# Sums of weights formed in DRAM, and six up-projection tiles in seven products, in a hybrid transformer block

## The chip, the cores and the metric

The kernel runs on one core of a Trainium2 chip. The metric is device time in microseconds (us) of one execution, the median of several runs. Engines are called by their short names in the profile: PE is TensorE, DVE is VectorE, ACT is ScalarE, POOL is GpSimd, and SP is SyncE, which only issues transfers (DMAs).

## The reference

One layer on 512 tokens of width 1024, all in float32:

```python
h = x
hn = rms_norm(h, ln_mix);  z = hn @ w_in            # 1024 x 3590
o_a = diff_attention(...)        # 4 heads, ALiBi, chunk-causal, difference of two softmaxes
o_b = forgetting_attention(...)  # 6 heads, causal, cumulative log forget gate
o_c = chunk_attention(...)       # 6 heads, own and earlier chunks, relative bias
h = h + concat(o_a, o_b, o_c) @ w_out               # 1024 x 1024
u = rms_norm(h, ln_ffn) @ w_up                      # 1024 x 5632
c = conv_b + sum_j conv_w[j] * shift(u, 2 - j)      # causal, width 3, along the tokens
gate, val = split(c)                                # 2816 features each
h = h + (silu(gate) * val) @ w_down                 # 2816 x 1024
g = sigmoid(rms_norm(h, ln_ple) @ w_ple_gate)       # 1024 x 1024
out = h + (p @ w_ple_proj) * g
```

## The kernel before

Every float32 product is made of three matmuls on operands that are split into a high part (`hi`, float32r) and a rest (`lo`): hi*hi, hi*lo and lo*hi (`mm3`). A weight tile is loaded into a raw tile of 128 x 768 (or 512) floats; ACT copies it to `w_hi`, DVE subtracts that from the raw tile and writes `w_lo` (`split`).

**Attention.** A loop over the parts of `w_in` (A0b, A1, A1b, B0, B1, B2, C0, C1, C2) runs four units each, one for 128 tokens, and then eight units of the output projection (`wo`, half n = 0, then n = 1). These units are counted by `slot`, 4 to 47. Between the matmuls of a unit stand pieces of the attention of earlier heads, by a table of slots (`T`). PE's order is that of the program; the other engines are ordered by the tile framework's planner, which simulates a time line, unless an instruction is pinned. `prefetch` loads the weights of the next part at the end of a unit. Some rests are formed by DMA: ACT writes the negated high part and GpSimd's queue adds the raw tile to it (`B_l<-B_r`, `C_l<-C_r`, `wo_l<-wo_r`).

**MLP.** A feature tile f (0 to 21) is 128 gate features and 128 value features. Plain tiles (`up_plain`) take three raw tiles (768, 768, 512 columns) and 48 matmuls of 512 tokens. Tiles in `SEVEN` (5, 10, 15) are computed by a scheme with seven products of half-size blocks in place of eight (`up_seven`), 84 matmuls of 256 columns, from weights that are sums of blocks: 3584 columns in five raw tiles. The right sides (sums of normalized columns, `Xh`, `Xl`) are formed once. After a tile come the convolution taps, the silu and the product with the value (`ff_chain`), all on ACT and DVE. Two finished tiles make one `left`: the seven sums of halves that the down projection multiplies (`g_ah`, `g_al`, or `xh`, `xl` at the end).

The down projection runs in phases of 6, 6, 6 and 4 feature tiles (`PHASES`) and, in each, for two halves n of the columns, again in seven products (`Down.product`, `RIGHT`, `PRODUCTS`), which are accumulated in three PSUM banks X, Y, Z; DVE adds each to `h` (`add_h`). Phases 0 and 1 run between up tiles, phases 2 and 3 together at the end (d0 and d1), followed by the gate (`pg`).

**The sums of weights.** They are formed in SBUF. For an up tile in seven products, five raw tiles are loaded, GpSimd's queue adds further blocks by three accumulating loads (`add_of`) and GpSimd adds four pairs of blocks (`sum_of`). For a down phase and half four blocks are loaded (`a1`, `b1`, `b2`, `a2`), and GpSimd forms the four differences `t1` to `t4` between the products, in the raw tiles (`diff`).

**Order in the MLP.** Each piece is a `Task` with its engines and estimated times. PE's tasks keep the order in which they are written; the others are ordered by a small planner that knows rings of buffers (`raw` 6, `hi` 7, `conv` 10, `left` 3), latest times counted back from PE and a clock per engine. Loads are emitted as soon as what they depend on is emitted, in a fixed order, and SP executes them in that order. The order of up tiles and down products comes from `fill`, `downs` and `AHEAD`.

## Time and profile before

| | |
|---|---|
| time, median of 3 runs | 728.63 us (727.79 to 728.96) |
| the profiled execution's own time | 727.37 us |
| its span, first to last instruction | 725.6 us |
| granted TensorE clock, mean | 0.999 |
| PE / DVE / ACT / POOL busy | 705.8 / 556.3 / 394.1 / 267.3 us |
| HBM read / written | 74.19 / 4.21 MB |

In the profile an instruction is named by what it writes and reads, `out<-in,in`; L78 is the line of the helper through which most engines are called, so instructions are told apart by their tiles. `w_raw`, `w_hi`, `w_lo` are weight tiles, `u` the up products, `sX`, `sY`, `sZ` the banks of a tile in seven products, `dn_X`, `dn_Y`, `dn_Z` those of the down projection, `dn_a`, `dn_b`, `dn_t` the raw tiles of its last phase. A group's row gives the count behind x, then busy us, the mean ns of one, the idle time of the engine before them and what ended it. A queue's row gives packets, MB and the share of the time of 16 DMA engines.

### The profile page before, as it was taken

Reading aid. Unit: us, or ns where it says so; the run is one execution under the profiler, and the core shown is the slowest. Engines: PE = TensorE matmul, PEld = TensorE weight load, DVE = VectorE, ACT = ScalarE, POOL = GpSimd, SP = SyncE. Lnnn points to the kernel's source line nnn. Section 1 sums busy time; section 2 is a strip of 40 time slices with the busy share of each in tenths; the row PEclk is TensorE's granted clock in tenths of the full one; section 3 lists DMA queues with packets and bytes.
Section 4 is the critical chain, followed back from the end, with each engine's and each line's share of the span. In section 5 each row is a group of like instructions: output and inputs, shape, how many; then the busy total and the mean of one; then the engine's idle time right before and its main releaser. Section 6 shows DMA issues by size and latency. Waiting matters only on the chain. (4 is left out here: it accounts for less than half of the span.)

```text
span 725.6 us, 11877 instructions
## 1 busy us (share of the span) xinstructions
PE 705.8 (97%) x4218; PEld 632.3 (87%) x4218; DVE 556.3 (77%) x1091; ACT 394.1 (54%) x745; POOL 267.3 (37%) x355
## 2 busy tenths in 40 slices
PE   9998999999999999999999999999999999999997
PEld 8888989898999887889888899888998888899886
DVE  7678788887878855758879968787898779988552
ACT  6656775865766664565555544543444543544821
POOL 5676676756665640211101144031520004361400
PEclk9999999999999999999999999999999999999999
DMA  9454425514211135564545334552263322122531
GB/s 330 170 139 110 124 59 124 138 30 110 88 53 52 59 66 167 170 208 90 144 138 125 101 97 122 142 156 66 88 178 114 95 87 83 57 73 93 159 126 58
DMA packets 36950, 83.22 MB, mean 115 GB/s; under 512 B 4214, under 2 KB 6262, under 8 KB 36892
## 3 DMA queue, kind: packets, MB, share of 16 engines
q1 hardware_dynamic: 32844, 73.52, 32.4%
q0 software_dynamic: 3760, 8.66, 6.4%
q8 instruction: 33, 0.54, 0.3%
q10 hardware_dynamic: 288, 0.30, 0.1%
q14 instruction: 25, 0.20, 0.1%
HBM read 74.19 MB, written 4.21 MB: 108 GB/s over the span
## 5 line engine op out<-in xcount | busy, mean ns | idle before, releaser
L78 DVE TENSOR_TENSOR w_lo<-w_raw,w_hi 128x768 fp32r<-128x768 f32 (+1 forms) x118 | 114.4, 989 | 20.2 <-ACT w_hi L78 19.6
L78 ACT CAST w_hi<-w_raw 128x768 fp32r<-128x768 f32 (+1 forms) x118 | 89.6, 786 | 70.1 <-POOL w_raw L78 32.0
L78 PE MATMUL u<-Tl,w_hi 128*128 128x512 f32 (+1 forms) x336 | 125.5, 374 | 0.8 <-DVE Tl L78 0.8
L78 PE MATMUL u<-Th,w_hi 128*128 128x512 f32 (+1 forms) x336 | 125.6, 374 | 0.6 <-ACT pps L78 0.6
L78 PE MATMUL u<-Th,w_lo 128*128 128x512 f32 (+1 forms) x336 | 125.3, 373 | 0.0
L78 POOL TENSOR_TENSOR w_raw<-w_raw,w_raw 128x768 f32<-128x768 f32 (+1 forms) x30 | 54.3, 1833 | 145.2 <-DVE w_lo L78 113.8
L78 PEld LDWEIGHTS u<-Tl,w_hi 128*128 128x128 f32 x336 | 63.0, 188 | 13.1 <-DVE Tl L78 1.2
L78 PEld LDWEIGHTS u<-Th,w_hi 128*128 128x128 f32 x336 | 63.0, 188 | 12.9 <-ACT pps L78 1.0
L78 PEld LDWEIGHTS u<-Th,w_lo 128*128 128x128 f32 x336 | 63.0, 188 | 12.5
L78 DVE SCALAR_TENSOR_TENSOR c<-u,cols,c 128x511 f32<-128x511 f32 x76 | 56.6, 746 | 18.6 <-ACT c L78 17.4
L78 POOL DMA_DIRECT2D w_raw<-in_w_up_dram x9 | 7.9, 907 | 100.1 <-DMA w_raw<-in_w_up_dram 93.9
L78 ACT ACTIVATE c<-u,cols 128x512 f32<-128x512 f32 x38 | 29.5, 776 | 22.7 <-PE u L78 22.7
L78 PE MATMUL dn_X<-w_hi,g_ah 128*128 128x256 f32 x144 | 40.7, 282 | 0.3 <-DVE h L78 0.3
L78 PE MATMUL dn_X<-w_lo,g_ah 128*128 128x256 f32 x144 | 40.6, 282 | 0.3 <-DVE w_lo L78 0.3
L78 PE MATMUL dn_X<-w_hi,g_al 128*128 128x256 f32 x144 | 40.5, 281 | 0.0
L78 PE MATMUL B_z<-B_h,Th 128*128 128x384 f32 x96 | 34.5, 360 | 0.6 <-DVE B_zn L78 0.6
L78 PE MATMUL C_z<-C_h,Th 128*128 128x384 f32 x96 | 34.3, 357 | 0.0
L78 PE MATMUL B_z<-B_h,Tl 128*128 128x384 f32 x96 | 32.3, 337 | 0.0
L78 PE MATMUL B_z<-B_l,Th 128*128 128x384 f32 x96 | 32.3, 337 | 0.0
L78 PE MATMUL C_z<-C_h,Tl 128*128 128x384 f32 x96 | 32.3, 336 | 0.0
L78 PE MATMUL C_z<-C_l,Th 128*128 128x384 f32 x96 | 32.3, 336 | 0.0
L78 PEld LDWEIGHTS dn_X<-w_hi,g_ah 128*128 128x128 f32 x144 | 27.1, 188 | 0.9 <-ACT w_hi L78 0.5
(484 smaller groups left out, 2143.8 us busy)
## 6 DMA issues: line engine op xcount, KB each, us to landing
w_raw<-in_w_up_dram SPq DMA_DIRECT2D x50, 384.0 KB, 3.9
w_raw<-in_w_down_dram SPq DMA_DIRECT2D x24, 384.0 KB, 3.1
w_raw<-in_w_up_dram SPq DMA_DIRECT2D x22, 256.0 KB, 3.3
B_r<-in_w_in_dram SPq DMA_DIRECT2D x12, 384.0 KB, 3.1
C_r<-in_w_in_dram SPq DMA_DIRECT2D x12, 384.0 KB, 3.3
wo_r<-in_w_out_dram SPq DMA_DIRECT2D x16, 256.0 KB, 3.0
w_raw<-in_w_ple_gate_dram SPq DMA_DIRECT2D x16, 256.0 KB, 3.0
h<-in_x_dram SPq DMA_DIRECT2D x4, 512.0 KB, 7.7
```

Of the source, the lines that this page charges most:

```text
L78: ins = getattr(self.eng, op)(*a, **k)
```

## The change

The sums of weights are formed in DRAM, by DMA alone. For each of ten sums (an up tile in seven products, or a down phase) a DRAM tile of four blocks is filled by four copies from the inputs (`copy_sum`, on SP's queue, in slots 8 to 43 of the attention) and three accumulating transfers from GpSimd's queue (`add_sum`: two blocks get the other addends, then block 1 is added to block 0, and block 0 to block 3). The sums that are needed first (up tiles 4, 7, 9 and phase 0) are added in slots 22 to 38, the others behind feature tiles 0 to 15 in the MLP (`late_sum`), each after a one-column GpSimd operation on the finished tile. The MLP then loads finished sums: `sum_of`, `add_of`, `again` and `diff` are gone, and a down phase and half loads seven raw tiles instead of four.

Six up tiles (4, 7, 9, 11, 13, 15) are computed in seven products instead of three (5, 10, 15). The order of up pieces (P plain, S seven) and down products (D) in the MLP is written out as a string. The seven products of the down projection use sums with other signs and in another order, with `add_h` adding or subtracting, and the left sums follow. `pool` and `sp` name the same engines as `nc.gpsimd` and `nc.sync`, through a wrapper that remembers the last instruction. The inputs hold the blocks in a matching layout (`w_usum`, `w_dsum`, `w_dadd`).

```diff
-AHEAD = 2
-SEVEN = (5, 10, 15)
+ORDER = ("PPPPSSPSSSPSPPPPSSPSSSPSPSSPSSSPSPDDDDDDDDDDDDDDSSPSSSPSPSSPSSSPSPSSPSSSPSPDDDDDDDDDDDDDDPPPPPPPPPPPPPPPPP")
+def tiles_of(order):
+    f, n, tiles = 2, {"P": 0, "S": 0}, {"P": [], "S": []}
+    for c in order:
+        if c in n:
+            if n[c] == 0:
+                tiles[c].append(f)
+                f += 1
+            n[c] = (n[c] + 1) % {"P": 3, "S": 6}[c]
+    assert f == NF and not any(n.values()), (f, n)
+    return tiles["P"], tiles["S"]
+EARLY_SUMS, FIRST_SUM, LAST_SUM = 11, 22, 16
+PLAIN, SEVEN = tiles_of(ORDER)
+_sums = sorted([(f, "u", f) for f in SEVEN] + [(PHASES[ph + 1] + 3, "d", ph) for ph in range(len(PHASES) - 1)])
+COPIES, ADDS, LATE = {}, {}, {}
+_late = [q for q in _sums if q[0] >= EARLY_SUMS]
+for _i, _q in enumerate(_sums):
+    for _k in range(4):
+        COPIES.setdefault(8 + (4 * _i + _k) * 36 // (4 * len(_sums)), []).append((_q[1:], _k))
+for _i, _q in enumerate(q for q in _sums if q not in _late):
+    for _k in range(3):
+        ADDS.setdefault(FIRST_SUM + _i // 3 * 10 + _i % 3 + 3 * _k, []).append((_q[1:], _k))
+for _i, _q in enumerate(_late):
+    for _k in range(3):
+        LATE.setdefault((3 * _i + _k) * LAST_SUM // (3 * len(_late)), []).append((_q[1:], _k))
...
+    DSUM, USUM, SUMS = {}, {}, {}
+    def sums_of(key):
+        if key not in SUMS:
+            if key[0] == "d":
+                ph = key[1]
+                DSUM[ph] = dp.tile([P, 4, 2, w_down[ph].shape[4]], F32, tag=f"dsum{ph}", name=f"dsum{ph}")
+                SUMS[key] = DSUM[ph], w_dsum[ph], w_dadd[ph]
+            else:
+                f = key[1]
+                USUM[f] = dp.tile([P, 4, 512], F32, tag=f"usum{f}", name=f"usum{f}")
+                SUMS[key] = USUM[f], w_usum[f], w_up[f][:, 1024:2048].rearrange("p (i c) -> p i c", i=2)
+        return SUMS[key]
+    def copy_sum(key, k):
+        v, src, _ = sums_of(key)
+        with tc.issue_after(sp.last):
+            nc.sync.dma_start(out=v[:, k], in_=src[:, k])
+    def add_sum(key, k):
+        v, _, more = sums_of(key)
+        to, src = ((v[:, 1:3], more), (v[:, 0], v[:, 1]), (v[:, 3], v[:, 0]))[k]
+        pool.dma_start(out=to, in_=src, accum_op=ALU.add, max_dma_last_dim=6144)
+    def next_job():
+        for q in COPIES.get(slot, ()):
+            copy_sum(*q)
+        for q in ADDS.get(slot, ()):
+            with tc.issue_after(pool.last):
+                add_sum(*q)
...
             slot += 1
+            next_job()
...
-    PRODUCTS = ((L1A, 0, "X", True), (L1, 4, "Y", True), (L2, 5, "X", False), (L4, 2, "Y", False),
-                (L3, 6, "X", False), (L2A, 1, "Z", True), (L2B, 3, "X", False))
+    PRODUCTS = {"1e": (0, "X", True, 1, 0, ALU.add), "S1": (3, "Y", True, 0, 1, ALU.subtract), "S2": (4, "X", False, 0, 0, ALU.add),
+                "1o": (2, "Z", True, 1, 0, ALU.add), "1e2e": (5, "X", False, 0, 1, ALU.subtract), "1oS2": (1, "Y", False, 0, 0, ALU.add),
+                "2o": (6, "X", False, 1, 1, ALU.subtract)}
...
-        ws = [tile_of(n, f"ws{f}_{i}", w_up[f][:, 768 * i : 768 * i + n]) for i, n in enumerate(size)]
-        src = w_up[f]
-        a = [add_of(ws[2], 512, 768, lambda: src[:, 1024:1280]), add_of(ws[3], 0, 768, lambda: src[:, 1280:2048])]
-        sums = [(2, 0, 2, 512), (2, 256, 3, 0), (3, 256, 2, 512), (3, 512, 3, 0)]
-        a += [sum_of(ws[i], c0, ws[j], c1, H, a) for i, c0, j, c1 in sums]
-        b = [add_of(ws[4], 0, 512, lambda: src[:, 2048:2560])]
-        for w, deps in zip(ws, ((), (), a, a, b)):
-            split_of(w, deps)
-        order = (0, 1, 4, 3, 5, 6, 2)
+        usum = USUM[f].rearrange("p i c -> p (i c)")
+        ws = [tile_of(n, f"ws{f}_{i}", w_up[f][:, 768 * i : 768 * i + n] if i < 2 else usum[:, 768 * (i - 2) : 768 * (i - 2) + n],
+                      deps=SUM_TASKS.get(("u", f), ()) if i > 1 else ()) for i, n in enumerate(size)]
+        for w in ws:
+            split_of(w)
+        order = (0, 1, 4, 3, 6, 5, 2)
...
-        raw = {what: tile_of(m, f"{name}_{what}", src.get(what), tag) for what in ("a1", "b1", "b2", "t2", "a2")}
...
+        src = {f"{c + 1}{'eo'[i]}": w_down[ph][n, i, c] for i in range(2) for c in range(2)}
+        src.update({what: DSUM[ph][:, i, n] for i, what in enumerate(("S2", "S1", "1e2e", "1oS2"))})
+        return lambda what: split_of(tile_of(m, f"{name}_{what}", src[what], tag, SUM_TASKS.get(("d", ph), ()) if what in ("S2", "S1", "1e2e", "1oS2") else ()))
...
+        for q in LATE.get(len(done_f) - 1, ()):
+            late_sum(f, *q)
...
+    LAST_X, SUM_TASKS = [], {}
+    tok = mp.tile([P, 1], F32, tag="tok", name="tok")
+    def late_sum(f, key, k):
+        b, slot = done_f[f]
+        def do():
+            pool.tensor_scalar(tok, G[f][:, 0:1], 1.0, 1.0, ALU.mult, ALU.mult)
+            add_sum(key, k)
+        SUM_TASKS.setdefault(key, []).append(Task("add", [("pool", 1.2), ("acc", (6, 4, 4)[k] + (8 if key[0] == "d" else 3))], do, (b, *SUM_TASKS.get(key, ())), (), [slot]))
...
+    FIRST = ("1e", "S1", "1o"), ("1e", "S1")
+    def down_pieces():
         for ph in range(2):
-            if ph not in due and all(f in done_f for f in range(PHASES[ph], PHASES[ph + 1])):
-                due[ph] = 0
-
-    def fill(n):
-        for _ in range(n):
-            at_f[0] = next(plain, NF)
-            pieces[0] += 1
-            if pieces[0] % 3 == 0:
-                count()
-
-    def downs(after=3):
-
-        for ph in range(2):
-            if due.get(ph, -1) >= after:
-                due[ph] = -99
-                for n in range(2):
-                    down(ph, n, DT)
-
-    for f in SEVEN:
-        while at_f[0] < f - AHEAD:
-            fill(1)
-            if pieces[0] % 3 == 0:
-                downs()
-        for i, _ in enumerate(up_seven(f)):
-            if i in (1, 4, 5):
-                fill(1)
-        count()
-        downs()
-    while at_f[0] < NF:
-        fill(1)
-        if pieces[0] % 3 == 0:
-            downs()
-    downs(0)
+            for n in range(2):
+                d = Down((ph,), n, DT)
+                for what in PRODUCTS:
+                    d.product(what)
+                    yield
+        for n, whats in enumerate(FIRST):
+            DL.append(Down((2, 3), n, ({"X": "z", "Y": "s", "Z": "o"} if n else DT)))
+            for what in whats:
+                DL[n].product(what, (2,), False)
+                yield
+    DL = []
+    pieces = {"P": (f for f in PLAIN for _ in up_plain(f)), "S": (f for f in SEVEN for _ in up_seven(f)), "D": down_pieces()}
+    for c in ORDER:
+        next(pieces[c])
...
+    d0, d1 = DL
+    for what in PRODUCTS:
+        d0.product(what, (3,) if what in FIRST[0] else None)
+    d1.product("1e", (3,))
     cols3(0, 0)
     cols3(1, 0)
-    d1.product("a1", (3,))
+    d1.product("S1", (3,) if "S1" in FIRST[1] else None)
     cols3(2, 0)
-    d1.product("a2")
     cols3(3, 0)
-    for what in ("t1", "t2", "b2", "t3"):
+    for what in ("S2", "1o", "1e2e", "1oS2"):
         d1.product(what)
+    d1.product("2o")
     cols3(0, 1)
     cols3(1, 1)
-    d1.product("t4")
```

131 lines of the change are left out of this document (42 added, 89 removed).

## The prediction

> **What bounds the kernel now.** I read the share of each engine first, then the stretches by stage, then who made TensorE wait, then the chain of the work that ended last. The first rows are the engines over the whole span; below them each row is one stretch: its length, the busy time of each engine, the granted clock, the DMA engines' mean busy share and GB/s.
>
> ```profile
> span 725.6 us, 11877 instructions
> PE 705.8 (97%) x4218; PEld 632.3 (87%) x4218; DVE 556.3 (77%) x1091; ACT 394.1 (54%) x745; POOL 267.3 (37%) x355
> ...
> core 0: us, PE busy (x) PEld busy (x) DVE busy (x) ACT busy (x) POOL busy (x), PEclk, DMA share, GB/s
> 60.00:115.00 55.00, 51.50 (x336) 47.94 (x335) 44.54 (x122) 38.27 (x86) 36.53 (x51) 1.00 0.47 119
> 115.00:230.00 115.00, 113.14 (x694) 107.09 (x693) 94.55 (x305) 76.26 (x184) 74.33 (x114) 1.00 0.29 81
> 230.00:290.00 60.00, 58.71 (x308) 50.07 (x307) 37.80 (x94) 34.67 (x80) 23.65 (x35) 1.00 0.34 92
> 325.00:430.00 105.00, 105.00 (x595) 91.02 (x595) 85.10 (x122) 56.30 (x85) 18.41 (x18) 1.00 0.43 112
> 430.00:460.00 30.00, 30.00 (x254) 29.96 (x253) 24.47 (x32) 12.42 (x17) 9.64 (x5) 1.00 0.52 155
> 460.00:515.00 55.00, 55.00 (x281) 46.17 (x280) 43.94 (x63) 27.74 (x42) 12.33 (x10) 1.00 0.36 96
> 515.00:545.00 30.00, 29.66 (x250) 29.49 (x249) 26.45 (x33) 12.32 (x17) 9.89 (x5) 1.00 0.52 156
> 545.00:620.00 75.00, 75.00 (x327) 60.40 (x326) 62.41 (x86) 34.02 (x51) 10.16 (x5) 1.00 0.32 96
> 620.00:676.00 56.00, 53.72 (x445) 52.63 (x444) 48.16 (x61) 26.70 (x42) 20.05 (x11) 1.00 0.24 76
> ```
>
> TensorE is the bound nearly everywhere, at full granted clock. From 325 to 676 us, the MLP, it is busy for all but 0.34 us (515 to 545) and 2.28 us (620 to 676). So a matmul taken out of the MLP is time gained, as long as nothing else becomes late. The attention (60 to 290) loses 3.50 + 1.86 + 1.29 = 6.65 us, and GpSimd is busy there for 74.33 of 115 us in the long middle stretch: the room for new work of its own is smallest in that place.
>
> **The products.** The change turns six feature tiles instead of three into seven-product tiles. The chain gives the price of each kind of matmul:
>
> ```profile
> 545.45 50.41 PE u L78 x216
> ...
> 646.02 5.30 DVE w_lo L78 x3
> ...
> 660.27 3.56 PE dn_X L78 x30
> ```
>
> A 128x512 product (u) takes 50.41 / 216 = 0.2334 us, a 128x256 one (dn_X, the shape of the seven products too) 3.56 / 30 = 0.1187 us. A plain up tile is 2 halves x 8 blocks x 3 products of 512 columns, 48 x 0.2334 = 11.20 us. A seven-product tile is 7 x 4 x 3 = 84 of 256 columns, 9.97 us. Each tile that moves saves 1.23 us, three save 3.7 us. The number of down products stays (7 per phase and half); only their order and signs change. Nothing covers these matmuls, so I count the whole 3.7.
>
> **GpSimd's sums and VectorE beside them.** The change removes from the MLP every sum and difference of weights that GpSimd forms in SBUF, and the nine accumulating loads of raw tiles. What these cost now is to be seen on VectorE. Forms of 325 to 676 us on VectorE (count, busy us, mean ns), GpSimd's accumulating loads (ns least/median/most), and single instructions in order of time:
>
> ```profile
> L78 DVE TENSOR_TENSOR w_lo<-w_raw,w_hi 128x768 fp32r<-128x768 f32 x87 | 92.2, 1076 | 12.3 <-ACT w_hi L78 11.9
> L78 DVE TENSOR_TENSOR w_lo<-dn_a,w_hi 128x512 fp32r<-128x512 f32 x8 | 8.4, 1058 | 0.5 <-ACT w_hi L78 0.3
> L78 DVE TENSOR_TENSOR sm<-c 128x256 f32<-128x256 f32 x11 | 6.3, 569 | 0.1
> L78 DVE TENSOR_TENSOR su<-sX,su 128x256 f32<-128x256 f32 x12 | 4.8, 419 | 8.4 <-ACT su L78 8.3
> ...
> L78 POOL DMA_DIRECT2D w_raw<-in_w_up_dram x9: 857/872/1185, 326.0 to 474.2; - x9
> ...
> 601.50 2.06 DVE L78 TENSOR_TENSOR sm<-c 128x256 f32<-128x256 f32 x1
> 622.79 0.42 DVE L78 TENSOR_TENSOR sm<-c 128x256 f32<-128x256 f32 x1
> 613.36 0.69 DVE L78 TENSOR_TENSOR c<-c,c 128x512 f32<-128x512 f32 x1
> 612.49 0.95 DVE L78 TENSOR_TENSOR w_lo<-w_raw,w_hi 128x768 fp32r<-128x768 f32 x1
> 613.96 2.61 DVE L78 TENSOR_TENSOR w_lo<-w_raw,w_hi 128x768 fp32r<-128x768 f32 x1
> 613.57 2.18 POOL L78 TENSOR_TENSOR w_raw<-w_raw,w_raw 128x768 f32<-128x768 f32 x1 [8.29 <-issue]
> ```
>
> The same low-half subtraction takes 0.95 us alone and 2.61 us beside a GpSimd sum; `sm` 0.42 and 2.06. So VectorE waits for GpSimd's sums. Over the MLP that is 87 x (1.076 - 0.95) = 11.0 us in the 768-column splits, 8 x (1.058 - 0.69) = 2.9 in those of dn_a, 11 x (0.569 - 0.42) = 1.6 in one kind of `sm`: at least 15 us of VectorE time that goes.
>
> What comes back on VectorE: a seven-product tile splits 3584 columns of weights, a plain one 2048. That is two more 768-column splits (1.9 us) and four `su` additions (4 x 0.42 = 1.7), 3.6 us for each of three tiles, 10.8 us in all. The balance is about 4 us less VectorE work, spread over 351 us in which it is busy for 290.5 (the sum of the six MLP rows, 83%). A pair of one seven-product and one plain tile lasts 11.2 + 10.0 = 21.2 us on TensorE; the existing pairs show how full VectorE is there:
>
> ```profile
> 409.00:430.20 21.20, 21.20 (x134) 18.97 (x133) 15.41 (x23) 11.09 (x18) 6.78 (x4) 1.00 0.22 61
> 493.70:514.80 21.10, 21.10 (x133) 18.89 (x132) 15.71 (x22) 10.16 (x16) 5.84 (x3) 1.00 0.18 51
> ```
>
> 15.5 of 21.1 us, with some of the pair's work left for later: the down weights' work follows at 24.47 of 30 us. Three such pairs now stand in a row twice, so I cost this at nothing, covered by 5 us of VectorE room per pair; without that cover the price is up to 3.6 us a pair.
>
> **The stalls in the down stages.** 0.34 + 2.28 = 2.62 us of TensorE idle time. The chain shows where most of it is made: three 768-column splits took 5.30 us at 646.02, against 3 x 0.95 = 2.85 alone, and TensorE's own waits name VectorE:
>
> ```profile
> PE dn_Y L78 <- DVE w_lo L78: 1.2, 1, 1.2
> PE wo L78 <- DMA wo_l<-wo_r: 0.9, 1, 0.9
> PE n_t L78 <- DVE h L78: 0.8, 1, 0.8
> PE C_s L78 <- POOL C_k_k L398: 0.4, 1, 0.4
> ```
>
> `dn_Y` waits 1.2 us for a split beside GpSimd's difference, `n_t` 0.8 for an addition queued behind the 5.30. With the differences gone these two go: 2.0 us. The other 0.6 stays. At the end the order changes too: d1's last product now stands ahead of the last transposes (cols3(0, 1), cols3(1, 1)) rather than behind them, so VectorE's split of them has no product of 3.56 us to hide in. The gate's first blocks use the other half of the columns; four blocks of three products (12 x 0.2334 = 2.8 us) cover ACT's copy and the split (0.69 us by the 512-column row). Zero, at most 1 us.
>
> **The sums in DRAM.** There are ten sums: six of up tiles of 1.05 MB, three of down phases of 3.15 MB, one of 2.10 MB, 17.8 MB in all. Each is four copies on SP's queue (40, at slots 8 to 43) and three accumulating transfers of the same total size from GpSimd. Twelve of these (three up tiles and phase 0, 6.3 MB) stand at slots 22 to 38; eighteen (11.5 MB) follow feature tiles 0 to 15 in the MLP, each behind a one-column GpSimd operation that waits for the tile. Further, loads grow: three more loads per down phase and half (8.7 MB) and 0.79 MB for each of three tiles. No transfer from DRAM to DRAM is in the trace. The rows are the queues, three kinds of issues (KB each, us to landing), the load and the first product of C0's weights, and the page's GB/s in 40 equal slices:
>
> ```profile
> q1 hardware_dynamic: 32844, 73.52, 32.4%
> q0 software_dynamic: 3760, 8.66, 6.4%
> ...
> w_raw<-in_w_up_dram POOLq DMA_DIRECT2D x3, 384.0 KB, 6.3
> B_l<-B_r POOLq DMA_DIRECT2D x5, 384.0 KB, 5.9
> C_r<-in_w_in_dram SPq DMA_DIRECT2D x12, 384.0 KB, 3.3
> ...
> 105.19 3.32 SPq L124 DMA_DIRECT2D C_r<-in_w_in_dram  x2
> 164.18 0.73 PE L78 MATMUL C_z<-C_h,Th 128*128 128x384 f32 x1
> ...
> GB/s 330 170 139 110 124 59 124 138 30 110 88 53 52 59 66 167 170 208 90 144 138 125 101 97 122 142 156 66 88 178 114 95 87 83 57 73 93 159 126 58
> ```
>
> C0's first unit, slot 28, starts at 164.18; at some 7 us a unit slots 22 and 38 lie near 120 and 235 us, so I use the row of 115 to 230 us. One MB costs 0.324 x 725.6 / 73.52 = 3.2 us of all 16 engines on SP's queue and 0.064 x 725.6 / 8.66 = 5.4 us on GpSimd's. From 115 to 230 us the copies are 8.7 MB (27.7 us) and the sums 6.3 MB (33.7 us); with the 33.4 us now busy (0.29) that is 95 of 115 us. It fits, but what lands in 3.3 us now will land later. Covered by lead: the attention's weights are loaded far ahead (C_r at 105.19 for products from 164.18 on). Not covered: SP's queue runs in order, so a bias or a late wo tile waits behind a copy of up to 0.79 MB (2.5 us), and wo_l already stops TensorE for 0.9 us in the output projection, where the last copies run.
>
> GpSimd's own price is 0.87 us an issue by the nine issues above, 12 x 0.87 = 10.5 us on an engine that is busy for 74.33 of 115 us: 74%. Behind each issue queue the scaling of probabilities and the moves of keys, which TensorE waits for only 0.4 us now. Bounds for the attention: nothing, or even 1 us gained by another order (that the planner reorders the unpinned engines excludes neither sign), up to all 10.5 us laid bare. I take 2 us: one copy's 2.5 us is seldom in the way and a fifth of the issues is nearer to the 0.4 us row than to all of them. In the MLP GpSimd has nothing else to do, the sums stand many tiles ahead of their loads, and the one-column operation is waited for by nobody but its sum: zero; if a sum came late, SP's loads behind it would stop too, 4 to 8 us each.
>
> **The sum.** -3.7 (products) - 2.0 (stalls) + 2.0 (attention) = -3.7 us. The profiled execution took 727.4 us, which is 1.2 below the median of the runs, 728.63; taken from the median, 724.9 us. I say 724.9.
>
> **The rivals.**
> *Transfers fill the DMA engines in the attention.* Slower. If a MB from DRAM to DRAM costs more than (115 - 33.4) / 61.4 = 1.33 times what the queues show now, the transfers of 115 to 230 us no longer fit. At 1.75 times they need 33.4 + 107.4 = 141 us, 26 late; with some 15 us of lead of the weights TensorE stands for about 11 us: 728.6 - 5.7 + 11 = 734 us. For it: the accumulating queue already costs 1.7 times SP's per MB. Against it: only loads queued behind copies suffer, and the copies have no early reader. Chance 0.13. The trace's fullest slice, the first, moved 330 GB/s. The Trainium skill (HBM Reference, Specifications (TRN2)) gives about 358 GB/s as a core's effective share; an estimate by it: 9.3 MB of now (81 GB/s), copies read and written (17.4) and sums read twice and written once (18.9) are 45.6 MB, 127 us in place of 115, which is this rival again; by the queues' own price it fits. No run here shows yet which holds.
> *GpSimd's issues lie bare.* Slower. With 10.5 us exposed, 728.6 - 5.7 + 10.5 = 733 us; it decides from 7.2 us on. The wait row of 0.4 us speaks against it. Chance 0.07.
> *The attention eats the gain.* A cost of 4.2 to 7.2 us: 728 us, no change. Chance 0.10.
> *VectorE becomes the bound in the pairs.* 3.6 us a pair for three pairs not covered: 728.6 - 3.7 + 10.8 - 5 of slack + 2 = 733 us. Against it the 15 us that GpSimd's sums give back. Chance 0.04.
> *The stalls stay.* They were not GpSimd's: 728.6 - 3.7 + 2 = 726.9, just faster. It is inside the forecast's 0.66.
>
> **How the numbers follow.** Faster or slower by 0.2% (1.46 us) is about what a measurement of this kernel can tell. Forecast 0.66 (721.5 to 727.1), no change 0.10, slower 0.24 (0.13 + 0.07 + 0.04). The low end takes all 2.62 us of stalls, 3.7 for products and 1 us of luck in the attention, 721.3, rounded to 721.5. The high end reaches into the slower cases until about 1 in 10 lies above: 733.
>
> **What would show it.** Right: `u` matmuls fewer by 144 and 252 more of 256 columns; the 768-column split at 0.95 us on average; TensorE busy without gaps from 325 us to the end of the down stage; the stage ahead of 290 us no more than 2 us longer. Wrong: TensorE waits in the attention for a bias, a wo tile or GpSimd; a DMA share near 1 from 115 to 230 us; loads in the MLP that wait for a sum.

## The result, and the profile after

The changed kernel takes 740.71 us (median of 4 runs, 739.88 to 741.33); the kernel before, beside it, 728.21 us. The ratio is 1.0173, with a 95% interval of 1.0158 to 1.0188: slower by 12.5 us, where 3.7 us less was forecast. The profiled execution took 741.33 us with a span of 739.6 us.

The first view is the page of the changed kernel: the engines, two DMA queues and the memory traffic.

```profile
span 739.6 us, 12254 instructions
...
PE 707.6 (96%) x4326; PEld 638.0 (86%) x4326; DVE 545.2 (74%) x1109; ACT 403.0 (54%) x763; POOL 221.2 (30%) x353
...
DMA packets 50569, 127.56 MB, mean 172 GB/s; under 512 B 5670, under 2 KB 7334, under 8 KB 50508
...
q1 hardware_dynamic: 42924, 102.36, 42.3%
q0 software_dynamic: 7296, 24.12, 18.7%
...
HBM read 118.49 MB, written 39.86 MB: 214 GB/s over the span
```

VectorE and GpSimd have less to do than before (545.2 against 556.3 us, 221.2 against 267.3), TensorE about the same, and the span is 14.0 us longer. Where it went shows in the start of two products: the first up product, which begins the MLP, and the first gate product, which ends it. The rows are those of the changed kernel, then of the kernel before (count, ns least/median/most, first and last start).

```profile
L111 PE MATMUL u<-Th,w_hi x288: 276/394/497, 332.7 to 636.2; 128*128 128x512 f32 x112, 128*128 128x256 f32 x32
...
L111 PE MATMUL pg<-w_hi,Th x28: 392/396/482, 689.3 to 711.2; 128*128 128x512 f32 x28
```

```profile
L78 PE MATMUL u<-Th,w_hi x336: 277/394/445, 313.4 to 618.8; 128*128 128x512 f32 x136, 128*128 128x256 f32 x32
...
L78 PE MATMUL pg<-w_hi,Th x28: 392/396/483, 675.5 to 697.3; 128*128 128x512 f32 x28
```

Ahead of the MLP 332.7 - 313.4 = 19.3 us are lost. The first addition is issued at 128.47 us; a product that starts shortly before it is the first `B_q_p` (the changed kernel, then the kernel before):

```profile
L111 PE MATMUL B_q_p<-ident,B_zn x12: 270/272/328, 125.7 to 187.7; 128*128 128x128 f32 x12
```

```profile
L78 PE MATMUL B_q_p<-ident,B_zn x12: 270/272/327, 121.6 to 170.0; 128*128 128x128 f32 x12
```

So 125.7 - 121.6 = 4.1 of the 19.3 us lie ahead of every addition. From there to the first up product it takes 332.7 - 125.7 = 207.0 us in place of 313.4 - 121.6 = 191.8: 15.2 us are lost behind it. The MLP lasts 689.3 - 332.7 = 356.6 us in place of 362.1: 5.5 us won. What follows lasts 50.3 in place of 50.1. So the change does in the MLP what it says, and pays 3.5 times as much for it ahead of the MLP.

Stretches of the changed kernel (length, busy time of each engine, granted clock, DMA share, GB/s):

```profile
20.00:62.00 42.00, 37.14 (x222) 34.24 (x220) 28.05 (x82) 23.52 (x55) 26.63 (x41) 0.92 0.63 203
...
115.00:230.00 115.00, 101.20 (x591) 92.36 (x590) 86.99 (x280) 66.51 (x163) 73.86 (x109) 0.97 0.78 193
130.00:140.00 10.00, 8.77 (x56) 8.05 (x54) 8.27 (x13) 7.10 (x13) 8.83 (x11) 1.00 0.93 197
140.00:150.00 10.00, 9.29 (x56) 8.10 (x56) 9.62 (x48) 6.75 (x20) 7.73 (x13) 1.00 1.03 265
150.00:160.00 10.00, 6.68 (x36) 5.06 (x34) 5.01 (x16) 3.43 (x10) 3.29 (x6) 1.00 1.03 297
160.00:170.00 10.00, 6.10 (x29) 5.91 (x30) 5.05 (x21) 3.74 (x10) 5.47 (x9) 0.66 0.45 123
...
180.00:190.00 10.00, 7.39 (x45) 6.64 (x44) 8.13 (x12) 4.38 (x9) 7.61 (x8) 1.00 0.97 213
190.00:200.00 10.00, 9.57 (x58) 8.45 (x57) 8.56 (x31) 4.77 (x14) 6.59 (x11) 1.00 1.09 285
```

From 115 to 230 us TensorE is busy for 101.20 us in place of 113.14. The mean DMA share is 0.78, a little under the 95 of 115 us that was worked out. But it isn't spread: for 30 us, from 130 to 160, and again from 180 to 200 the DMA engines are full. The chain of the work that ended last runs through the first of these stretches:

```profile
142.81 17.38 DMA bias_B<-fk_d
...
162.19 1.05 POOL B_rs L111
...
163.26 0.50 DVE B_zn L111
...
163.90 1.30 PE B_z L111 x3
```

One bias of 256 KB, which landed in 3 to 4.5 us before, took 17.38 us. GpSimd wants it for the diagonal (`dg`); behind that stand, in its order, an addition's issue and the norm's small operations (`B_rs`), VectorE's scaling and then TensorE's projection. The timeline of the SP queue shows what the bias was issued among, GpSimd's timeline the addition that began at the same time and the stop behind the bias:

```profile
139.53 0.50 SPq L841 DMA_DIRECT2D dsum<-in_w_dsum_dram  x1
140.12 1.38 SPq L111 DMA_DIRECT2D C_r<-in_w_in_dram  x1
141.55 0.88 SPq L841 DMA_DIRECT2D dsum<-in_w_dsum_dram  x1
142.81 4.83 SPq L561 DMA_DIRECT2D bias_B<-fk_d  x2
```

```profile
142.87 1.24 POOL L111 DMA_DIRECT2D dsum<-in_w_dadd_dram  x1
...
160.31 0.63 POOL L566 TENSOR_SCALAR_AFFINE_SELECT dg<-bias_B 128x512 f32<-128x512 f32 x1 [6.60 <-DMA bias_B<-fk_d]
```

The addition of 142.87 is phase 0's first, 1536 KB. The copies are issued right behind the loads of C's weights, which run ahead of their unit, so that copies, loads, the bias and the additions of two sums meet there.

### The profile page after: what moved, and what is told of

Same layout as the page of the kernel before. It is cut to its first block, busy times and chain, and to the rows that moved or that the text cites. A ratio compares the mean times of both kernels' runs of the same rounds, so it can differ in the third digit from the quotient of the medians.

```text
span 739.6 us, 12254 instructions
## 1 busy us (share of the span) xinstructions
PE 707.6 (96%) x4326; PEld 638.0 (86%) x4326; DVE 545.2 (74%) x1109; ACT 403.0 (54%) x763; POOL 221.2 (30%) x353
## 2 busy tenths in 40 slices
DMA packets 50569, 127.56 MB, mean 172 GB/s; under 512 B 5670, under 2 KB 7334, under 8 KB 50508
## 3 DMA queue, kind: packets, MB, share of 16 engines
q1 hardware_dynamic: 42924, 102.36, 42.3%
q0 software_dynamic: 7296, 24.12, 18.7%
## 4 chain that ended last, share of the span: by engine, by line
PE 72%; DVE 10%; DMA 7%; POOL 5%; issue 3%; ACT 2%; SPq 0%; POOLq 0%; DVEq 0%; ACTq 0%
PE u L111 22%; PE dn_X L111 8%; PE pg L111 6%; PE C_z L111 5%; PE wo L111 4%; PE dn_Y L111 4%; PE sX L111 3%; PE B_z L111 2%; DMA bias_B<-fk_d 2%; PE sY L111 2%; PE dn_Z L111 2%; PE sZ L111 2%; POOL B_rs L111 1%; DMA h<-in_x_dram 1%; PE pp L111 1%
## 5 line engine op out<-in xcount | busy, mean ns | idle before, releaser
L111 ACT CAST w_hi<-w_raw 128x768 fp32r<-128x768 f32 (+1 forms) x124 | 94.4, 788 | 59.7 <-PE dn_X L111 19.9
L111 DVE TENSOR_TENSOR w_lo<-w_raw,w_hi 128x768 fp32r<-128x768 f32 (+1 forms) x124 | 109.0, 902 | 20.8 <-ACT w_hi L111 20.6
L111 PE MATMUL u<-Th,w_hi 128*128 128x512 f32 (+1 forms) x288 | 106.9, 371 | 0.8 <-DVE su L111 0.8
L111 PE MATMUL u<-Tl,w_hi 128*128 128x512 f32 (+1 forms) x288 | 106.5, 370 | 0.8 <-DVE Tl L111 0.8
L111 PE MATMUL u<-Th,w_lo 128*128 128x512 f32 (+1 forms) x288 | 106.3, 369 | 0.0
L111 POOL TENSOR_SCALAR tok<-c 128x1 f32<-128x1 f32 x18 | 9.2, 513 | 211.4 <-DVE c L111 211.3
L111 DVE SCALAR_TENSOR_TENSOR c<-u,cols,c 128x511 f32<-128x511 f32 x64 | 47.7, 747 | 22.5 <-ACT c L111 21.5
L111 PEld LDWEIGHTS u<-Th,w_hi 128*128 128x128 f32 x288 | 54.0, 188 | 10.6 <-DVE su L111 1.1
L111 PEld LDWEIGHTS u<-Th,w_lo 128*128 128x128 f32 x288 | 54.0, 188 | 10.5 <-DVE w_lo L111 0.2
L111 PEld LDWEIGHTS u<-Tl,w_hi 128*128 128x128 f32 x288 | 54.1, 188 | 10.4 <-DVE Tl L111 1.2
```

The costliest lines, as they stand in the source:

```text
L111: ins = getattr(self.eng, op)(*a, **k)
```

## The experiments

A result with no interval is one run beside one run of the kernel before; such runs are read by their stages, not by differences of 0.3%. "First `B_q_p`" and "first up product" are the starts of the rows shown above, "between" is the time from the one to the other, "the MLP" the time from the first up product to the first gate product. They are read from the one execution that was profiled.

**What the parts cost: no sums, copies alone, small additions.** In the first kernel there are no copies and no additions, in the second no additions; in the third the early additions move 64 columns of a row each.

```diff
-                DSUM[ph] = dp.tile([P, 4, 2, w_down[ph].shape[4]], F32, ...)
+                DSUM[ph] = w_dsum[ph]
-                USUM[f] = dp.tile([P, 4, 512], F32, ...)
+                USUM[f] = w_usum[f]
...
-            copy_sum(*q)
-        for q in ADDS.get(slot, ()):
-            with tc.issue_after(pool.last):
-                add_sum(*q)
+            sums_of(q[0])
...
-        for q in LATE.get(len(done_f) - 1, ()):
-            late_sum(f, *q)
```

> Copies, additions and the one-column operations are left out; the loads take unsummed blocks of the inputs, so the sums of weights are missing from the result. Theory A (the transfers of the sums fill the DMA engines in the attention): the attention is back at its time before, the MLP keeps its 5.4 us: 723 us. Theory B (GpSimd's twelve issues hold up its other work): the same 723 us. Theory C (the tile framework's planner orders the attention worse, with or without the transfers): 735 us or more.

```diff
-        for q in ADDS.get(slot, ()):
-            with tc.issue_after(pool.last):
-                add_sum(*q)
...
-        for q in LATE.get(len(done_f) - 1, ()):
-            late_sum(f, *q)
```

> The forty copies stay, all additions and one-column operations are left out; the loads take unsummed copies, so the sums are missing from the result. Theory A: copies alone take 17.8 MB x 3.1 us = 55 us of DMA time spread over 240 us that are 35% busy; they fit apart from some bunches: 725 to 730 us. Theory B: all issues are gone, 723 us. If the copies ahead of the loads on SP's queue make the loss by themselves: 737 to 740 us.

```diff
+        if small:
+            cut = (slice(None),) * (1 + (key[0] == "d" and k == 0)) + (slice(0, 1),) * (key[0] == "d" or k == 0) + (slice(0, 64),)
+            to, src = to[cut], src[cut]
...
-                add_sum(*q)
+                add_sum(*q, small=True)
```

> The twelve additions of the attention stay in place with the same number of descriptors, but each moves only 64 columns of a row, a 24th to an 8th of the bytes; so most of those sums are missing from the result. Theory A (bytes on the DMA engines): the loss is that of the copies alone, 723 to 726 us. Theory B (the issues on GpSimd, 12 x 0.9 us, and what queues behind them): 735 to 740 us.

| kernel | us (before beside it) | first `B_q_p` | first up product | between | MLP | longest landing of a bias |
|---|---|---|---|---|---|---|
| before | 728.21 | 121.6 | 313.4 | 191.8 | 362.1 | 4.5 |
| no sums | 721.22 (730.44) | 122.5 | 314.6 | 192.1 | 354.2 | 5.0 |
| copies alone | 722.38 (730.44) | 124.0 | 315.8 | 191.8 | 354.2 | 9.2 |
| early additions of 64 columns | 728.64 (728.50) | 126.1 | 319.2 | 193.1 | 357.4 | 10.1 |
| changed | 740.71 (728.21) | 125.7 | 332.7 | 207.0 | 356.6 | 17.4 |

The row of 115 to 230 us in these three, in this order:

```profile
115.00:230.00 115.00, 112.88 (x691) 106.54 (x691) 93.91 (x304) 75.76 (x184) 73.79 (x114) 1.00 0.27 82
```

```profile
115.00:230.00 115.00, 112.57 (x688) 105.80 (x687) 94.24 (x307) 76.09 (x184) 73.06 (x112) 1.00 0.54 166
```

```profile
115.00:230.00 115.00, 112.16 (x682) 104.25 (x681) 95.12 (x305) 75.93 (x184) 82.37 (x121) 1.00 0.59 168
```

The times between the two products tell the parts. With no transfers it is 0.3 us more than before. The forty copies alone add nothing, at a DMA share of 0.54. The additions with a few columns each add 1.3; they make as many packets as the full ones (7296 on GpSimd's queue), GpSimd is busy for 82.37 us and TensorE hardly notices (112.16). The bytes of the twelve early additions add 207.0 - 193.1 = 13.9. The 728.64 us lie between what the two theories asked for, and nearer to that of the bytes.

The 4.1 us ahead of the first `B_q_p` can't be divided so well. The last three kernels of the table execute the same instructions in the same order there, and still reach it at 124.0, 126.1 and 125.7 us. The kernel before with six tiles (below), whose attention is that of the kernel before, reaches it at 123.1, 1.5 us later. So single executions differ there by some 2 us, and only the rest can be put down to the copies.

The kernel without sums also shows that the new order of the products isn't at fault, which had been a rival of mine: its MLP is 7.9 us shorter than before, and the late additions take only 2.4 of that back (356.6 against 354.2).

**Is it SP's queue?** The biases were moved to the queue of ACT, where no copy stands ahead of them:

```diff
-            nc.sync.dma_start(out=tb, in_=bias_c[hd])
+            nc.scalar.dma_start(out=tb, in_=bias_c[hd])
...
-            nc.sync.dma_start(out=tb, in_=bass.AP(fk_d.tensor, ...
+            nc.scalar.dma_start(out=tb, in_=bass.AP(fk_d.tensor, ...
```

> The loads of bias_B and bias_C are issued on ACT's queue in place of SP's, so that they stand behind no copy; nothing else. Theory A, place in the queue: bias_B lands within 6 us rather than 17, the stall of 6.5 us and the half clock behind it go: 729 to 733 us. Theory A, full engines whatever the queue: bias_B still lands after 10 us or more, 736 to 740 us. Theory B: 740 us.

736.82 us (before beside it 730.44); first up product at 328.2, 203.4 us behind the first `B_q_p`. A bias still takes up to 12.0 us to land on a queue of its own, as the theory of the full engines asked for, and a new wait of 3.2 us comes at 173.9 us. By this one execution the place in the queue is worth 207.0 - 203.4 = 3.6 of the 15.2 us; the rest isn't the queue's order.

**Later in the attention.** The early additions start at slot 30 in place of 22, in the second kernel with the biases on ACT's queue besides:

```diff
-EARLY_SUMS, FIRST_SUM, LAST_SUM = 11, 22, 16
+EARLY_SUMS, FIRST_SUM, LAST_SUM = 11, 30, 16
```

> The twelve additions of the attention stand eight slots later (30 to 46), behind the heads of B, whose bias tables are read back from DRAM. Theory A: the bunch of additions, copies and weights from 130 to 162 us is split, bias_B lands within 9 us, the stall of 6.5 us goes; some loss comes back at the tables of C: 728 to 734 us. Theory B: the same number of issues in a stretch where GpSimd is as busy: 737 to 741 us.

> As the run with the additions eight slots later, and the bias tables are loaded on ACT's queue. Theory A: 1 to 4 us faster than that one, since the tables of C then stand behind no copy either: 726 to 731 us. If the engines are full whatever the queue: no difference between the two.

738.45 and 738.22 us (728.50); first up product at 328.4 and 329.3, 204.0 and 203.9 us behind the first `B_q_p`. Both miss the range of the theory of the bytes. The first lies in that of GpSimd's issues (737 to 741), which the small additions had ruled out. The long bias of 142 us is gone (8.9 at most in the first), and others take its place. TensorE's waits in the first of the two:

```profile
PE wo L111 <- DMA wo_l<-wo_r: 4.0, 2, 3.7
PE C_z L111 <- DVE C_zn L111: 2.9, 1, 2.9
```

A bias of C's maps took 7.88 us there and a low half of the output projection's weights came 3.7 us late. At either place in the attention some reader near the additions has no lead.

**Into the MLP.** Phase 0's additions behind feature tiles 0 and 1, ahead of the late ones (first kernel), or the late sums' copies on GpSimd's queue in the MLP (second):

```diff
-EARLY_SUMS, FIRST_SUM, LAST_SUM = 11, 22, 16
+EARLY_SUMS, FIRST_SUM, LAST_SUM = 11, 22, 14
...
-_late = [q for q in _sums if q[0] >= EARLY_SUMS]
+_late = [q for q in _sums if q[0] >= EARLY_SUMS or q[1] == "d"]
```

> The three additions of phase 0's sum (3.1 MB) move from the attention to feature tiles 0 and 1; its copies stay, and the later sums follow one or two feature tiles sooner or later than now. Theory A: the 16 us in which its first addition keeps the DMA engines busy are gone, the worst bunch is halved: 728 to 733 us. Theory B: three of twelve issues fewer, a quarter of the loss: 736 us.

```diff
-            copy_sum(*q)
+            sums_of(q[0])
+            if q[0] not in [w[1:] for w in _late]:
+                copy_sum(*q)
...
+            if k == 0:
+                v, src, _ = sums_of(key)
+                for j in range(4):
+                    pool.dma_start(out=v[:, j], in_=src[:, j])
```

> The copies of the six late sums (11.5 MB) leave the attention; they are issued in the MLP on GpSimd's queue, ahead of each sum's first addition. The attention keeps 6.3 MB of copies and all its additions. Theory A, copies and additions together fill the engines: the first product of the MLP starts at 318 to 322 us rather than 332.7. Theory A, the additions alone do it: at 328 us or later. The MLP may become later if its sums are too slow: 0 to 10 us.

752.89 us (730.44) and 744.08 us (728.50). The first misses both of its ranges. In its attention a bias still takes 14.3 us to land (first up product at 327.0), and it loses 17.2 us of MLP (373.8 against the changed kernel's 356.6). GpSimd waits long there for the steps of a sum, which follow one another, and TensorE for VectorE:

```profile
POOL dsum L111 <- DMA dsum<-in_w_dadd_dram: 33.2, 3, 12.3
```

```profile
PE u L111 <- DVE su L111: 9.5, 2, 4.7
```

That the one comes of the other isn't shown: at 445 us, ahead of one of these waits, the chain runs from TensorE's own `sX` through ACT's rounding and VectorE's splits to `su`.

The second gains in the attention: the first up product comes at 323.9, 198.5 us behind the first `B_q_p`, 8.5 less than in the changed kernel and between what its two theories asked for. It has one gap of 8.87 us, which ends at 527.6 us, behind a load that stood in SP's order behind a late sum:

```profile
507.31 12.52 DMA usum<-usum
...
520.32 6.39 DMA w_raw<-in_w_up_dram
```

That the move of copies helped by 8.5 us where copies alone cost nothing says that the two kinds make each other worse; the next two runs ask how far.

**Cut, or kept apart.** Phase 0's three additions in eight pieces; then the additions as they were, with the early sums' copies at slots 8 to 20 and the late sums' at 36 to 47.

```diff
+        if _q[1] == "u":
+            ADDS.setdefault(FIRST_SUM + _i // 3 * 10 + _i % 3 + 3 * _k, []).append((_q[1:], _k))
+for _j in range(8):
+    ADDS.setdefault((23, 24, 26, 27, 30, 31, 34, 36)[_j], []).append((("d", 0), _j))
```

> The changed kernel with phase 0's three additions (1536, 768 and 768 KB) cut into eight of 384 KB each, at slots 23, 24, 26, 27, 30, 31, 34 and 36; the same bytes, five issues more (some 6 us more of GpSimd). Theory A1 (bunching: one addition of 1536 KB occupies the DMA engines for 16 us, and the loads that need their data at once wait that long): the longest landing of a bias falls from 17.4 us to under 10, the 6.5 us wait at 163.9 us goes, and the first up product comes at 322 to 327 us instead of 332.7, 730 to 735 us in all. Theory A2 (each byte costs, however it is cut): first up product at 331 us or later, 739 us or more.

```diff
-        COPIES.setdefault(8 + (4 * _i + _k) * 36 // (4 * len(_sums)), []).append((_q[1:], _k))
+        _j = 4 * [q for q in _sums if (q in _late) == (_q in _late)].index(_q) + _k
+        COPIES.setdefault(36 + _j // 2 if _q in _late else 8 + _j * 13 // 16, []).append((_q[1:], _k))
```

> The changed kernel with the copies taken out of the additions' way: the sixteen copies of the early sums at slots 8 to 20, the twenty-four of the late sums at slots 36 to 47 (after the additions), the additions untouched. Theory A3 (the 19 us come from copies, loads of C's weights and additions meeting at 130 to 160 us, each of which alone would fit): the bias lands in under 10 us, first up product at 320 to 325 us, 728 to 733 us in all. Theory A2 (the additions' bytes themselves, whatever stands beside them): first up product at 329 us or later, 737 us or more.

Cutting does nothing: 740.62 us (727.92), ratio 1.0180 (1.0162 to 1.0198), first up product at 331.1, 207.2 us behind the first `B_q_p`, a bias of 18.0 us. My theory that one large addition makes the stretch full fell. Keeping the copies apart gives 738.79 us (727.83), ratio 1.0140 (1.0111 to 1.0169); in the profiled execution the first up product comes at 326.4, 202.3 us behind the first `B_q_p`, and no bias takes 8 us. The row of 115 to 230 us, of the pieces and of the copies apart:

```profile
115.00:230.00 115.00, 103.45 (x596) 94.91 (x596) 86.87 (x284) 66.61 (x166) 77.81 (x115) 0.94 0.78 183
```

```profile
115.00:230.00 115.00, 107.58 (x648) 99.33 (x647) 92.90 (x298) 72.21 (x177) 78.78 (x117) 1.00 0.64 146
```

In that execution 207.0 - 202.3 = 4.7 of the 13.9 us are gone. But it was the fastest of four, 734.77 us against 738.44 to 739.53 for the others. By the medians keeping the copies apart gains 740.71 - 738.79 = 1.9 us, the intervals of the two ratios overlap, and the time is the one that the theory of the bytes had asked for (737 or more). So how much comes of copies and additions meeting stays open, somewhere from 2 to 5 us; the larger part stays with the additions, at a mean share of 0.64 and with no bias late.

**Do the products pay without sums in DRAM?** The kernel before, with the six tiles of the change:

```diff
-SEVEN = (5, 10, 15)
+SEVEN = (4, 7, 9, 11, 13, 15)
```

> The kernel before with six up tiles in seven products (4, 7, 9, 11, 13, 15) and every sum still formed in SBUF by GpSimd: the products' part of the change alone, with no transfer from DRAM to DRAM. Theory A (the change lost by the transfers of its sums in the attention, and the products' gain is real): the attention is as before, the first up product at 313 to 314 us, and the MLP is shorter by at most 3 x 1.23 = 3.7 us, about 725 to 726 us in all, since GpSimd's sums of three more tiles (about 10 us of GpSimd each) slow VectorE's splits further. Rival (the sums in SBUF leave no room, VectorE becomes the bound in the pairs and that is what the change was needed for): TensorE waits for VectorE in the MLP, 728 us or more.

740.93 us (727.96), ratio 1.0175 (1.0158 to 1.0192); in the profiled execution, the slowest of four (743.12 us), the MLP takes 375.9 us, 13.8 more than before. TensorE's waits there, and the 768-column splits:

```profile
PE u L78 <- DVE c L78: 5.8, 3, 4.4
PE sX L78 <- DVE su L78: 2.6, 3, 1.5
```

```profile
L78 DVE TENSOR_TENSOR w_lo<-w_raw,w_hi 128x768 fp32r<-128x768 f32 x95 | 101.0, 1075 | 16.2 <-ACT w_hi L78 15.6
```

The rival was right: with GpSimd's sums in SBUF the splits stay at 1.075 us and VectorE is late. Part of it is the place of the first of the six: the longest wait (4.4 us at 351 us) stands where VectorE still forms the differences of the activations. Another choice of six tiles wasn't tried.

**Mixtures.** The sums of tiles 4, 7, 9 and of phase 0 in SBUF, the late ones in DRAM; then phase 0's alone in SBUF; then seven-product tiles 11, 13, 15, 17, 19, so that every addition is late (phase 0 in SBUF). The functions that sum in SBUF are those of the kernel before.

```diff
+IN_SBUF = [("u", 4), ("u", 7), ("u", 9), ("d", 0)]
...
-            copy_sum(*q)
-        for q in ADDS.get(slot, ()):
-            with tc.issue_after(pool.last):
-                add_sum(*q)
+            if q[0] not in IN_SBUF:
+                copy_sum(*q)
```

> The changed kernel with the sums of its first three seven-product tiles and of phase 0 formed in SBUF by GpSimd as in the kernel before: no addition from DRAM to DRAM is left in the attention, and sixteen of the forty copies go (those of the four early sums); the six late sums stay in DRAM, their copies in the attention. Theory A (the twelve early additions cost the attention 13 us by the bytes that they move, 3 more by their issues and descriptors; copies and late sums cost 1 to 3 each): the first up product comes at 315 to 316 us instead of 332.7, the MLP takes 356 to 359 us, and the time is 724 to 727 us, faster than the kernel before. Rival (any traffic of the sums in the attention, copies too, stops TensorE and halves its clock afterwards): first up product at 320 us or later and a time of 730 us or more.

```diff
+IN_SBUF = [("d", 0)]
...
         for q in ADDS.get(slot, ()):
-            with tc.issue_after(pool.last):
-                add_sum(*q)
+            if q[0] not in IN_SBUF:
+                with tc.issue_after(pool.last):
+                    add_sum(*q)
```

> The changed kernel with phase 0's sums alone formed in SBUF by GpSimd as in the kernel before, its four copies and three additions left out; the sums of the first three seven-product tiles stay in DRAM, added in the attention (nine additions of 3.1 MB), so that half of the attention's added bytes and the largest of them go. Theory A1 (the one large sum makes the bunches): first up product at 318 to 322 us, the MLP 357 to 360 us, and 726 to 731 us in all. Theory A2 (cost by the byte): 10 us of the 19.4 stay, first up product at 323 us or later. Against both stands what the kernel with all four early sums in SBUF showed (first up product at 313.6, but gaps in the MLP behind GpSimd's sums and a load of 10.1 us beside an addition): if phase 0's sums in SBUF are what stops the MLP, it takes 365 us or more.

```diff
-ORDER = ("PPPPSSPSSSPSPPPPSSPSSSPSPSSPSSSPSPDDDDDDDDDDDDDDSSPSSSPSPSSPSSSPSPSSPSSSPSPDDDDDDDDDDDDDDPPPPPPPPPPPPPPPPP")
+ORDER = ("PPPPPPPPPPPPPPPPPPPPPPPPPDDDDDDDDDDDDDDSSPSSSPSPSSPSSSPSPSSPSSSPSPDDDDDDDDDDDDDDPPSSPSSSPSPSSPSSSPSPPPP")
...
+IN_SBUF = [("d", 0)]
```

> The changed kernel with its seven-product tiles moved to 11, 13, 15, 17 and 19 (five in place of six; 2 to 10 are plain), so that every sum in DRAM is late: eight sums, 24 additions of 14.7 MB behind feature tiles 0 to 15; phase 0's sums, now among plain tiles, in SBUF by GpSimd; their copies (32) in the attention as before. Theory A (the additions cost where the data of the attention's loads are needed at once; in the MLP the loads have lead and room): first up product at 314 to 316 us; the MLP 358 to 361 us (2 tiles x 1.23 us = 2.5 less for products, some 2 to 4 less of stalls, 2 to 3 more for the additions); 724 to 727 us, faster than before by 0.2 to 0.5%. Rival (an addition costs TensorE the same wherever it runs): the MLP gives back what the attention gains, 370 us or more of MLP, 735 us or more in all.

| kernel | us (before beside it) | ratio, 95% interval | first up product | between | MLP |
|---|---|---|---|---|---|
| four early sums in SBUF | 738.91 (727.96) | 1.0157, 1.0125 to 1.0190 | 313.6 | 192.1 | 377.4 |
| phase 0 in SBUF | 745.36 (727.92) | 1.0226, 1.0172 to 1.0280 | 322.2 | 198.8 | 372.6 |
| late tiles | 737.32 (727.83) | 1.0133, 1.0112 to 1.0155 | 315.7 | 193.4 | 370.2 |

The profiled executions took 742.84, 746.99 and 737.98 us, so that the first two MLPs are some us longer here than in the median.

In the attention all three went as the theory of the bytes says: 192.1 and 193.4 us with no addition there, 198.8 with half of the bytes, which is 7.0 of the 15.2 us. In the MLP all three missed: I had expected 356 to 361. The chain of the first, with GpSimd's timeline beside it, and then the chain of the third:

```profile
394.17 10.10 DMA w_raw<-in_w_up_dram
```

```profile
392.65 1.19 POOL L112 DMA_DIRECT2D dsum<-in_w_dadd_dram  x1 [0.26 <-issue]
407.45 0.92 POOL L112 DMA_DIRECT2D w_raw<-in_w_up_dram  x1 [13.61 <-DMA w_raw<-in_w_usum_dram]
```

```profile
456.81 12.58 DMA w_raw<-in_w_up_dram
```

Beside the additions these up weights need 10 to 13 us to land. In the changed kernel no such load stops TensorE in the MLP; with GpSimd's sums between load and product (407.45: GpSimd idle for 13.61 us until the load is there) the lead is gone. So an addition can cost in the MLP too, where a reader has lost its lead. How much of the three MLPs is due to that wasn't separated: the six tiles with every sum in SBUF took 375.9 us with no addition at all.

The third kernel had a rival, that an addition costs TensorE the same wherever it runs, and both of its numbers came true (370 us or more of MLP, 735 or more in all). Its mechanism did not. Two stretches of the MLP:

```profile
470.00:560.00 90.00, 89.66 (x618) 82.72 (x616) 73.77 (x110) 47.17 (x74) 11.13 (x18) 1.00 0.80 209
...
625.00:645.00 20.00, 15.20 (x100) 14.26 (x99) 15.62 (x25) 10.86 (x17) 0.00 (x0) 0.84 0.64 207
```

In the first, nine additions are issued and the DMA engines are as busy as in the attention, and TensorE loses 0.34 of 90 us. In the second it loses 4.8 of 20, and the last addition was issued at 577.10 us.

No version with all its sums beat the kernel before.

## Why the prediction was wrong

**Products, -3.7 us: right.** Per product kind the up matmuls fall from 336 to 288, 144 in all. The MLP became 5.5 us shorter, against -3.7 - 2.0 = -5.7 forecast for products and stalls together.

**GpSimd's sums and VectorE at nothing: right.** The splits of 768 columns in the MLP now take 0.954 us on average, as forecast (0.95):

```profile
L111 DVE TENSOR_TENSOR w_lo<-w_raw,w_hi 128x768 fp32r<-128x768 f32 x95 | 89.5, 954 | 14.7 <-ACT w_hi L111 14.5
```

The pairs aren't bound by VectorE (that rival fell), and the six tiles in SBUF show that this hangs on the sums' move: with these six tiles the gain of the products wasn't had without it.

**Stalls, -2.0 us: right.** No wait of the down stages is left; what remains of the MLP's waits over 0.3 us in one piece is 0.8 us each of `u` and `sX` behind `su`, and `u` behind `Tl` as before. The order at the end costs 0.2 us (0 taken, bound 1).

**Sums and waits in the MLP at nothing: nearly.** The additions there cost about 2.4 us, from the kernel without sums; against it stand 2 us more than forecast that the products and stalls gave (7.9 with no sums, 5.7 forecast). That the whole came out at 5.5 is in this part luck.

**The attention, +2.0 us: this step failed; it is +19.3.** The price of the bytes held: 0.423 x 739.6 / 102.36 = 3.06 us per MB on SP's queue and 0.187 x 739.6 / 24.12 = 5.73 on GpSimd's, against 3.2 and 5.4. So did their sum as a mean, 0.78 x 115 = 90 us of 115 against 95 (the same work now reaching past 230 us). What failed is "It fits" and what was hung on it: a mean over 115 us says nothing of 20 us in which everything meets. Of the two readers without lead that I named, I priced only the place in the queue, at one copy of 2.5 us; that is worth 3.6 us (the biases on a queue of their own). That the engines behind the queues are full is the larger part. By the experiments the 19.3 us are 4.1 ahead of the first addition, 1.3 in the small additions (their issues and packets) and 13.9 in the bytes of the early additions, of which some 2 to 5 go if the copies stand elsewhere. The 4.1 are there at 66 us already; copies of the early sums are issued there between the loads of the second projection (the stretch of 20 to 62 us above, at a share of 0.63 and a clock of 0.92), but some 2 us of it also come and go between executions. I had looked for nothing there.

**The bounds.** I let "all 10.5 us laid bare", GpSimd's issues, be the upper end of the attention. That was the wrong resource: issues and packets with few bytes cost 1.3. The end should have come from the transfers.

**The rivals.** *Transfers fill the DMA engines in the attention* was right in its mechanism and too small, 734 against 740.7 us. It also had a wrong condition: it was to decide from 1.33 times the queues' price, and it decided at 1.06 times (5.73 / 5.4). Beside it stood the 358 GB/s of the Trainium skill (HBM Reference, Specifications (TRN2)) as a limit. The same section of the Trainium skill says that a core streaming alone goes above this share, bounded by its DMA engines; I had left that out. This kernel runs on one core, and the trace agrees: the full stretches of 140 to 160 us moved 265 and 297 GB/s, and in 3.4 us it was 399, though a copy counts once there that reads and writes the memory (127.56 MB moved by DMA in all, 158.35 read and written):

```profile
157.80:161.20 3.40, 0.00 (x0) 1.00 0.99 399
```

What was full is the time of the DMA engines. *GpSimd's issues lie bare* fell: 1.3 us. *The attention eats the gain* was on the right side and too small. *The stalls stay* fell.

**What stays open.** How the larger part of the additions' 13.9 us comes about was not taken apart further. With the copies moved away single waits of 0.9 to 3.0 us are spread over the attention; the longest, for `wo_l`, stands where the moved copies run. The 4.1 us ahead of the first addition aren't explained beyond the scatter, and the MLPs of the mixtures aren't divided between GpSimd's sums, the additions and the order of the tiles. Additions without their copies weren't tried, since they would add to memory that nothing has written.

## What to carry to other kernels

A mean share of the DMA engines over a stage is no sign that a transfer is hidden: look for the 20 us where it will meet others, and for each small load there that is issued just ahead of its use, since a load beside accumulating transfers landed here up to four times as late (17.4 us in place of 4.5). The same share costs next to nothing where the loads have lead: 0.34 of 90 us at a share of 0.80 in the MLP. Give work that is moved from a full engine to the DMA engines a stage where all loads have that much lead. And two parts that only pay together (fewer products, sums elsewhere) are to be priced together, with the one's cost at its worst place.

## What was not expected of the hardware

**The granted clock falls to half after short waits.** Stretches of the changed kernel (TensorE's busy time is the first number behind the length, the clock the third from the end):

```profile
28.10:31.50 3.40, 1.32 (x8) 0.71 (x8) 3.36 (x13) 1.36 (x4) 2.82 (x4) 1.00 0.00 1
31.50:34.90 3.40, 3.09 (x15) 2.81 (x15) 3.40 (x8) 3.40 (x6) 1.16 (x2) 0.51 0.12 17
...
45.20:48.60 3.40, 1.56 (x10) 1.06 (x9) 1.85 (x6) 1.14 (x4) 3.19 (x4) 1.00 0.98 244
48.60:52.00 3.40, 3.40 (x14) 3.40 (x13) 2.77 (x5) 1.34 (x3) 2.57 (x5) 0.50 0.88 284
...
161.20:168.00 6.80, 4.10 (x15) 3.94 (x16) 3.63 (x17) 1.77 (x5) 3.99 (x7) 0.50 0.50 116
```

Twice TensorE was busy for 1.3 to 1.6 of 3.4 us, with single gaps of no more than 1.2 us, and got half the clock for the next 3.4; after 3.4 us with no matmul at all (157.8 to 161.2) and 3.4 more with 0.7 us of work it was 6.8 us. In the profiled execution before the change this happened only at the very end. The first of these stretches isn't the sums' doing, though: it has no transfer in it, and the kernel before with six tiles, which has no sum in DRAM, shows the same:

```profile
28.10:31.50 3.40, 1.54 (x12) 1.11 (x12) 3.32 (x13) 1.32 (x5) 2.83 (x4) 1.00 0.00 0
31.50:34.90 3.40, 3.27 (x14) 3.00 (x15) 3.40 (x9) 3.40 (x6) 1.36 (x2) 0.50 0.08 8
```

Nor do the runs give a limit: in the kernel with the copies apart 1.52 us of work from 282.7 to 286.1 us was followed by the full clock. A wait can so cost more than its own length: over the three stretches of the changed kernel at most (3.09 + 3.40 + 4.10) / 2 = 5.3 us, a part of the 19.3. The Trainium skill (TensorE: Matmul & The Clock Gate, What's actually happening) names a window of 3.4 us, which agrees; it asks for an idle one, and here a window with 1.3 to 1.6 us of work was followed by half the clock.

**An accumulating queue takes three quarters of the engines from a plain one beside it.** Counted from the trace's packet records of 149 to 157 us, while phase 0's first addition ran (share of 16 engines, packets of more than 4 bytes, in 2 us each):

```
149  addition 0.81, 54 packets   SP's queue 0.27, 46 packets
151  addition 0.79, 53 packets   SP's queue 0.26, 44 packets
153  addition 0.69, 46 packets   SP's queue 0.28, 47 packets
155  addition 0.83, 55 packets   SP's queue 0.25, 43 packets
```

The packets are about equal in number, 208 to 180; the addition's take longer, 0.78 x 16 x 8 / 208 = 0.48 us each against 0.265 x 16 x 8 / 180 = 0.19. Part of that is size: of the packets of 6144 bytes alone, the addition's took 0.48 us and those of SP's queue 0.25. The equal numbers agree with what the Trainium skill says (DMA: Bandwidth & Descriptors, Queues, rings and completion order), that each engine takes its queues in turn, a packet at a time. Why cutting the addition into pieces changed nothing it doesn't explain: the pieces' packets were half as large (3072 bytes; 7888 packets on GpSimd's queue in place of 7296) and the loss stayed.
